# Hybrid attention and Fourier encoder on one core: sink columns a period later, another order for the first Fourier tile, POOL for one operand, another pool for one gather

## The chip, the core and the metric

The kernel runs on one core of one Trainium2 chip. The metric is the device time of one launch in microseconds, the median of three runs. Five engines work side by side, each through its own instructions in order: PE (matrix products), ACT (scalar engine), DVE (vector engine), POOL (GpSimd) and SP, which here only issues DMAs. POOL and ACT issue some DMAs too.

## What is computed

Two sequences, 2048 and 512 positions of 1024 channels, pass through two layers and a last RMSNorm.

```python
def attention_layer(x, g, w_in, w_out, sink, rel_bias):
    h = rmsnorm(x, g); z = h @ w_in            # q, k, v, gate
    # per head: softmax over |i-j| <= 128 of q.k/8 + bias[i-j], with a sink logit in the denominator
    o = banded_gqa_with_sink(q, k, v, rel_bias, sink)
    return x + (o * silu(gate)) @ w_out

def fourier_layer(x, g, w_gate, w_out):
    h = rmsnorm(x, g)
    # per group of 256 channels: real part of the 2-D DFT over (positions, channels of the group)
    f = fftn(h in 4 groups, axes=(positions, channels), norm="ortho").real
    return x + (f * silu(h @ w_gate)) @ w_out
```

## The kernel before

**Numbers in two parts.** Every float32 operand of a matmul is kept as an upper part (a cast to fp32r, made by ACT) and a lower part (the rest, a subtraction by DVE or POOL). `matmul3` (line 94 carries its matmuls) adds three products of them into one bank of PSUM. `split` makes both parts of a tile.

**Attention.** The 2560 positions are worked off in five chunks of 512; chunk 0 is the short sequence. In a chunk, eight pairs of heads follow each other. A period, `n` in `range(17)`, covers half a pair: the scores of a new half (`scores`, L451), the transposes (`transp`, L509, tile `pt`), casts (`parts`, L517 on ACT and L518 on DVE, tile `pts`) and the product with v (`av`, L535) of the half before, with projections of later pairs (`qp`, `gp`) placed in between as filler for PE. The order inside a period is written out by hand: `seq` chains the instructions of PE, ACT and DVE in the order of the program, and `after` ties others to an anchor. A scheduler decides the rest of the order at build time; at run time each engine goes through its instructions strictly in that order.

At every even period `at[n // 2 + 1].start()` takes a bias tile `b` for the next pair: SP loads its 384 middle columns from `rowd` (L426), and at once ACT copies the negated sink logits into its first and last column (L431). The next instructions of ACT are casts of `pts`. DVE reads the tile first two periods after `start`, when it adds bias and scores (`biased`, L470). `out_evac` copies the upper half of the av result with ACT (L544, tile `t`) and finishes it with DVE and POOL (L553 to L559). `extra(i)` then issues side work, among it the squares of the next chunk's rows (L161). In chunk 0 the weights come in float32 (`w32q`, `w32g`, `w32o`) and are split on ACT (L113) and POOL (L118).

**Fourier layer, first part.** The 20 tiles of 128 positions are taken in pairs of tiles. For a pair (class `Pair`), `norms` squares and scales a tile, `turn` transposes half of it (L972), `own` and `parts` make the two parts, `sums` forms the sums of a Strassen-like scheme, `z` (L94, L1022) and `z_odd_even` (L1036, L1043) multiply by the channel DFT. `gates` then forms seven products with parts of the gate weights in three PSUM accumulators W, Z and X: B11, then X with `b21`, T1, T2, B22, T3 and N4; behind each, `hooks` do steps of the next pair. The first pair (tiles 16 and 17) has no pair ahead of it, so its steps stand by themselves behind the rest of the attention phase (`tail`): `turns1` and `turns2` (both tiles transposed, tile 17 first), `turns3`, `turns4`, `z_odd_even` of tile 17, `z` of tile 16. `build` loads `w32N` and splits it into N4 and T3, both lower parts on DVE (L914).

**Fourier layer, second part.** `position` forms the DFT over positions for two mirrored residues at a time, multiplies by the gate (`s2`, L1294) and gives two row tiles `u`. `gated` loads the gate rows: by SP, or for the mirrored residue by an indirect gather that POOL issues (L1243), into a tile of the pool `x` (four buffers, `xtile`). The last residues 1, 7, 3 and 5 go through class `Outs`; while `products` of one multiplies by the output weights, its hooks `split_g`, `transform` and `turns` prepare the next. `f_sums("N4", left)` loads four weight tiles into the pool `L` (20 buffers, `left`).

Of the kernel before, what the change touches and what calls it, by code (L numbers as in the profile page):

```python
# [37 lines left out]
def f32(ap):  # L38
    return ap.bitcast(F32)
# [3 lines left out]
def encoder(  # L43
# [97 lines left out]
    def attention_phase():  # L141

        with ExitStack() as es:
# [274 lines left out]
            def attention(c, p, res, uTs):  # L418
# [5 lines left out]
                def start():  # L424
                    bt = ap.tile([P, 2, 386], F32, tag="bias", bufs=2, name=f"b{c}_{p}")
                    SP.dma_start(  # L426
                        bt[:, :, 1:385],
                        bass.AP(rowd.tensor, rowd.offset + p * 1024, [[1, P], [512, 2], [1, 384]]),
                    )

                    ends = ACT.copy(bt[:, :, 0:386:385], sk[:, 2 * p : 2 * p + 2, None].to_broadcast([P, 2, 2]))  # L431
                    if p:
                        seq(ACT, ends)
                    st["bias"] = bt
                    uT = wp.tile([P, 2, CH], F32R, align_bytes=LINE, tag="uT", bufs=8, name=f"uT{c}_{p}")
                    uTs.append((uT[:, 0], uT[:, 1]))
                    st["uT"] = uT

                def span(b):
                    gb = tok // P + b  # L440
# [123 lines left out]

                    return split

                return start, scores, biased, exps, divide, transp, parts, av, out_evac

            def out_proj(c, uTs):
                tok = CHUNKS[c][0]  # L570
# [56 lines left out]
                steps.append(lambda: evac(1))  # L627
                return steps

            Heads = namedtuple("Heads", "start scores biased exps divide transp parts av out_evac")  # L630

            def pieces(out, a, b, op):

# [133 lines left out]
            for c in range(len(CHUNKS)):  # L767

                if c > 1:
                    hs, halo = make_h(c, invb)  # L770
                for s in tail:
                    s()
                if c == 1:
                    hs, halo = make_h(c, invb)
                if c:
                    invb0 = kv_proj(c, hs, halo)
                else:
                    invb0 = kv_proj(c, hs, halo, first_norms, early)
                rowd, sk = bias
                uTs = []  # L780
                res = [{} for p in range(8)]
                at = [Heads(*attention(c, p, res[p], uTs)) for p in range(8)]
                loads, work = [], []
                for p in range(8):
                    load, steps = qg_proj(c, p, hs, res[p], invb0)
                    loads.append(load)
                    work += steps
                loads[0]()
                at[0].start()

                ahead_n = 16 if c == 0 else 12
                chain.pop(PE, None)
                for s in work[:8]:
                    s()
                loads[1]()
                for s in work[8:ahead_n]:
                    s()

                m = 15 * KD - ahead_n
                quota = [m * (i + 1) // 27 - m * i // 27 for i in range(27)] + [4, 4]  # L800
                assert sum(quota) == len(work) - ahead_n
                work = work[ahead_n:]
                op = out_proj(c, uTs)
                split = None

                def extra(i):
                    nonlocal norm_steps, invb, inv
                    if c + 1 < len(CHUNKS):
                        if i == 24:
                            norm_steps = stats(c + 1)  # L810
                        if i >= (38 if c else 24) and i % (2 if c else 4) == 0 and norm_steps:
                            inv = norm_steps.pop(0)()
                        elif i == 56:
                            invb = spread(c + 1, inv)
                    if c in EXTRA and i in EXTRA[c]:
                        EXTRA[c][i]()
                    if c == len(CHUNKS) - 1 and i in AHEAD:
                        AHEAD[i]()
                    if c == 0 and i % 8 == 3 and 1 <= i // 8 < 3:
                        load_w(0, LATE[i // 8 - 1], f"late{i // 8}", late=last_exp[0])  # L820

                fourth = bank(f"s{c}")
                zeros(fourth)
                for n in range(17):
                    new = (at[n // 2], 2 * (n % 2)) if n < 16 else None
                    old = (at[(n - 1) // 2], 2 * ((n - 1) % 2)) if n else None
                    if n % 2 == 0 and n < 14:
                        at[n // 2 + 1].start()
                    if n % 2 and n // 2 + 2 < 8:
                        loads[n // 2 + 2]()  # L830
                    chain.setdefault(PE, None)

                    if new:
                        new[0].scores(new[1], spt[:2])
                    if old:
                        for b in range(2):
                            old[0].transp(old[1] + b)
                    if new:
                        for j in range(2):
                            new[0].biased(new[1], j)  # L840
                        new[0].scores(new[1] + 1, (spt[2], spt[0] if n else fourth))
                    if n == 15:

                        for j in range(2):
                            new[0].biased(new[1] + 1, j)
                    if old:
                        for b in range(2):
                            old[0].parts(old[1] + b)
                    if new:
                        for j in range(2):  # L850
                            new[0].exps(new[1], j)
                    if split and c:
                        split()
                        split = None
                    if new:
                        if n < 15:
                            for j in range(2):
                                new[0].biased(new[1] + 1, j)
                        while late:
                            late.pop()()  # L860
                        new[0].divide(new[1], 0)
                        for j in range(2):
                            new[0].exps(new[1] + 1, j)
                        new[0].divide(new[1], 1)
                        for j in range(2):
                            new[0].divide(new[1] + 1, j)
                    for i in range(quota[2 * n] if n < 15 else 18 - n):
                        (work or op).pop(0)()
                    if split:
                        split()  # L870
                        split = None
                    if old:
                        old[0].av(old[1])
                        split = old[0].out_evac(old[1])
                    for i in range(4 * n, 4 * n + 4):
                        extra(i)
                    if n == 16:
                        split()
                    half = quota[2 * n + 1] if n < 14 else 4 if n == 14 else 2
                    for i in range(half):  # L880
                        (work or op).pop(0)()
                chain.pop(PE)
                if c == len(CHUNKS) - 1:

                    for i in range(2):
                        op[i]()
                        op[i] = lambda: None
                tail = op
            return tail

    def fourier_phase(tail):
        with ExitStack() as es:
# [18 lines left out]
            def split(t, src, lo_engine=DVE):  # L911

                ACT.copy(t[:, 0], src)
                lo_engine.tensor_tensor(t[:, 1], src, f32(t[:, 0]), ALU.subtract)  # L914
                return t[:, 0], t[:, 1]

            def split_T(src, name, flip=False):
# [205 lines left out]
            def take(w32, k, place, *names):  # L1123

                for w, half in sorted(zip(names, range(2))):
                    wg[w][k] = split(place([P, 2, 512], F32R, f"w{w}_{k}"), w32[:, half])

            def build(k):
                w32 = right([P, 2, 512], F32, f"w32N_{k}")
# [70 lines left out]
            kept = []  # L1200

            pr = pairs[0]
            turns1(pr)
            turns2(pr)
            turns3(pr)
            turns4(pr)
            more()
            more()
            pr.z_odd_even()
            for hf in range(2):  # L1210
                pr.z(hf)
            for k in range(4):
                build(k)
            for n, pr in enumerate(pairs[:-1]):
# [391 lines left out]
            for k1, k2 in ((7, 3), (3, 5), (5, None)):  # L1606
# [1 line left out]
                gl, tb = nxt["r"]  # L1608

                def split_g():  # L1610
                    nxt["s"] = [gated(name, r, xtile) for r in tiles]
                    if not ft["N4"]:

                        f_sums("N4", left)
                    nxt["p"] = [halves_of(name, *gl, hf) for hf in range(2)]

                def transform(third):
                    nxt["o"] = Outs(k1, position(name, k1, None, None, tiles, (nxt["s"], tb), nxt["p"], third))

                def turns():  # L1620
# [109 lines left out]
```

## Time and profile before

| | |
|---|---|
| median of 3 runs | 1607.7 us (1604.67 to 1608.85) |
| profiled execution | 1608.11 us, span 1606.3 us |
| PE busy | 1586.9 us (99%) |
| DVE, ACT, POOL busy | 1141.7, 880.3, 438.2 us |
| DMA | 373.90 MB, 233 GB/s mean |
| mean granted PE clock | 0.997 |

Busy time is the time in which an engine has an instruction running; ends of matmuls are modelled, so short stops of PE may not show in it. In the timelines of the profile a row gives start, duration, engine, line, operation, tiles (out<-in), shape and count, and in brackets the idle time before it with what ended it. Buffer numbers are left out of the names: `trb` is any transpose bank of the first Fourier part, `jkb` the scratch output of a square, `x` a row tile.

### The profile page before, as it was taken

The page shows a single profiled execution, that of the slowest core. Times are in us where ns is not written, and L with a number is a line of the kernel's source. Part 1 is how long each engine was busy: PE and PEld are TensorE (multiplying, and loading weights), DVE is VectorE, ACT ScalarE, POOL GpSimd, SP SyncE. Part 2 cuts the span into 40 slices and gives each one's busy share as a digit, 9 for nine tenths or more (in the row PEclk, how much of TensorE's full clock was granted, in tenths as well). Part 3 has the DMA queues.
Part 4 walks back from the last instruction along what each step waited for, and adds up shares of the span by engine and source line. Part 5 has one row for each costly group of instructions (what it writes and reads, how often), then busy time and mean ns, then how long its engine had stood idle before and what let it go on. Part 6 is the DMA issues. An engine that isn't in the chain of part 4 may idle for free.

```text
span 1606.3 us, 27426 instructions
## 1 busy us (share of the span) xinstructions
PE 1586.9 (99%) x9755; PEld 1322.6 (82%) x9755; DVE 1141.7 (71%) x2779; ACT 880.3 (55%) x2107; POOL 438.2 (27%) x605
## 2 busy tenths in 40 slices
PE   9999999999999999999999999999999999999998
PEld 7776888888898888988888888878888887888886
DVE  6787665777538776377764577668878877888696
ACT  6687634677237674257752476646655554343352
POOL 2466561421403414024222242211112121100010
PEclk9999999999999999999999999999999999999999
DMA  7577696655765576756659656656657569455952
GB/s 291 207 286 263 226 349 233 227 220 205 289 230 191 206 257 235 251 194 229 238 164 334 211 208 222 243 201 225 217 203 248 184 224 407 166 185 206 352 192 92
DMA packets 100580, 373.90 MB, mean 233 GB/s; under 512 B 12139, under 2 KB 22379, under 8 KB 83036
## 3 DMA queue, kind: packets, MB, share of 16 engines
q1 hardware_dynamic: 81708, 297.91, 52.4%
q0 software_dynamic: 16400, 70.04, 11.3%
q10 hardware_dynamic: 2336, 4.20, 0.7%
q8 instruction: 78, 1.28, 0.3%
q14 instruction: 58, 0.48, 0.1%
HBM read 280.84 MB, written 91.26 MB: 232 GB/s over the span
## 4 chain that ended last, share of the span: by engine, by line
PE 83%; DMA 7%; DVE 5%; ACT 2%; issue 1%; POOL 1%; SPq 0%; POOLq 0%; DVEq 0%; ACTq 0%
PE qp L94 13%; PE gp L94 12%; PE op L94 9%; PE spt L94 8%; PE spt L451 6%; PE av L535 6%; PE W L94 5%; PE fo L94 4%; PE vp L94 4%; PE pt L509 3%; PE Z L94 3%; PE Wo L94 2%; PE X L94 1%; PE z L94 1%; DMA b<-rowd 1%
## 5 line engine op out<-in xcount | busy, mean ns | idle before, releaser
L470 DVE CUSTOM_DVE_ANT_0 S<-spt,b 128x385 f32<-128x385 f32 (+1 forms) x315 | 154.2, 528 | 121.1 <-PE spt L451 120.8
L94 PE MATMUL qp<-h,wq 128*128 128x512 f32 x960 | 238.6, 398 | 0.0
L94 PE MATMUL gp<-h,wg 128*128 128x512 f32 x960 | 237.4, 395 | 0.0
L94 PEld LDWEIGHTS gp<-h,wg 128*128 128x128 f32 x960 | 174.9, 188 | 43.3 <-issue 9.7
L94 PEld LDWEIGHTS qp<-h,wq 128*128 128x128 f32 x960 | 175.9, 189 | 41.8 <-issue 5.5
L478 ACT ACTIVATE S<-S 128x385 f32<-128x385 f32 (+1 forms) x320 | 190.3, 606 | 18.4 <-DVE S L470 17.0
L517 ACT CAST pts<-pt 128x384 fp32r<-128x384 f32 (+1 forms) x320 | 123.8, 472 | 131.1 <-PE pt L509 130.8
L518 DVE TENSOR_TENSOR pts<-pt,pts 128x384 fp32r<-128x384 f32 (+1 forms) x320 | 147.6, 523 | 34.5 <-ACT pts L517 33.6
L94 PE MATMUL op<-wo,uT 128*128 128x512 f32 x600 | 140.4, 391 | 0.0
L94 PE MATMUL fo<-wo,tTu 128*128 128x512 f32 x576 | 139.1, 392 | 0.0
L94 PEld LDWEIGHTS op<-wo,uT 128*128 128x128 f32 x600 | 111.9, 188 | 23.9 <-issue 0.7
L451 PE MATMUL spt<-kwin,qab 64*128 64x384 f32 (+1 forms) x945 | 129.5, 356 | 0.0
L559 POOL TENSOR_TENSOR uT<-o,uT 128x256 fp32r<-128x256 f32 x75 | 55.6, 741 | 250.5 <-ACT uT L558 246.2
L94 PEld LDWEIGHTS fo<-wo,tTu 128*128 128x128 f32 x576 | 106.3, 188 | 20.3
L535 PEld LDWEIGHTS av<-pts,v 128*128 128x128 f32 x576 | 101.0, 188 | 24.0 <-ACT pts L517 3.7
L535 PE MATMUL av<-pts,v 128*128 128x512 f32 (+1 forms) x576 | 117.0, 342 | 3.3 <-ACT pts L517 2.6
L451 PEld LDWEIGHTS spt<-kwin,qab 64*128 64x128 f32 x945 | 84.2, 185 | 29.9 <-issue 21.5
L490 DVE TENSOR_SCALAR S<-S 128x384 f32<-128x384 f32 (+1 forms) x192 | 91.4, 476 | 6.4
L555 POOL TENSOR_TENSOR o<-o,s 128x256 f32<-128x256 f32 x75 | 55.3, 738 | 134.4 <-DVE o L553 134.1
L94 PE MATMUL spt<-wo,uT 128*128 128x512 f32 x360 | 86.7, 392 | 0.0
L94 PEld LDWEIGHTS spt<-wo,uT 128*128 128x128 f32 x360 | 66.5, 188 | 13.7
L509 PEld LDWEIGHTS pt<-ident,S 64*128 64x128 f32 x1792 | 68.2, 138 | 5.2 <-issue 2.3
(317 smaller groups left out, 2985.8 us busy)
## 6 DMA issues: line engine op xcount, KB each, us to landing
wo<-wsd SPq DMA_DIRECT2D x32, 1024.0 KB, 5.9
wq<-wsd SPq DMA_DIRECT2D x31, 1024.0 KB, 7.6
wg<-wsd SPq DMA_DIRECT2D x31, 1024.0 KB, 5.1
x<-x1d SPq DMA_DIRECT2D x40, 512.0 KB, 3.7
b<-b21d SPq DMA_DIRECT2D x40, 512.0 KB, 6.5
b<-rowd SPq DMA_DIRECT2D x40, 384.0 KB, 4.3
xs<-in_x_dram SPq DMA_DIRECT2D x23, 512.0 KB, 6.7
s2d<-gt POOLq DMA_DIRECT2D x40, 256.0 KB, 3.2
```

The source lines that it names most:

```text
L94: pe(PE.matmul(out, a[i], b[j], start=start and i + j == 0, stop=stop and i == 1, skip_group_check=more))
L451: pe(PE.matmul(banks[j][:, 2 + k0 * P : 2 + k1 * P], res["q"][rows, qp, b * P : (b + 1) * P], kwin[g][rows, kp, b * P + k0 * P : b * P + k ...
L470: seq(DVE, DVE.tensor_tensor_reduce(out=s[:, e0:e1], in0=ps[:, 1 + e0 : 1 + e1], in1=st["bias"][:, j, 386 - e1 : 386 - e0][:, ::-1], scale ...
L478: last_exp[0] = seq(ACT, ACT.activation(s[:, e0:e1], s[:, e0:e1], AF.Exp, bias=s[:, 386:387], scale=-1.0, accum_out=s[:, 387:388]))
L490: seq(DVE, DVE.tensor_scalar(s[:, ks], s[:, ks], den, None, ALU.mult))
L509: pe(PE.transpose(ps[h][:, kb, j, :], ss[j][rows, 1 + kb * P : 1 + (kb + 1) * P], ident[rows, rows]))
L517: seq(ACT, ACT.copy(hi, ps[:, k0:k1]))
L518: seq(DVE, DVE.tensor_tensor(lo, ps[:, k0:k1], f32(hi), ALU.subtract))
L535: pe(PE.matmul(to, v, pt, start=n == part == 0, stop=part == 1 and n in (1, len(todo) - 1), skip_group_check=n > 1,))
L555: eng.tensor_tensor(o, o, s, ALU.mult)
L559: low = eng.tensor_tensor(lo, o, f32(hi), ALU.subtract)
```

## The change

Four edits. The sink copy leaves `start` and becomes a step of its own, `sinks`, which runs in the odd period after `start`, behind `out_evac` and ahead of `extra`. The first pair of the Fourier layer transposes tile 16 and forms its `z` ahead of tile 17's steps. The lower parts of N4 are made by POOL in two pieces each. In `split_g` the second tile of residue 7 comes from the pool `L`, and `f_sums("N4", left)` moves from `split_g` to `transform`.

```diff
@@ attention
-                    ends = ACT.copy(bt[:, :, 0:386:385], sk[:, 2 * p : 2 * p + 2, None].to_broadcast([P, 2, 2]))
-                    if p:
-                        seq(ACT, ends)
...
+                def sinks():
+                    ends = ACT.copy(
+                        st["bias"][:, :, 0:386:385], sk[:, 2 * p : 2 * p + 2, None].to_broadcast([P, 2, 2])
+                    )
+                    if p:
+                        seq(ACT, ends)
@@ ahead of period 0
                 at[0].start()
+                at[0].sinks()
@@ in period n
                         split = old[0].out_evac(old[1])
+                    if n % 2 and n < 15:
+                        at[n // 2 + 1].sinks()
                     for i in range(4 * n, 4 * n + 4):
                         extra(i)
@@ split
-                lo_engine.tensor_tensor(t[:, 1], src, f32(t[:, 0]), ALU.subtract)
+                for cs in (slice(0, 256), slice(256, 512)) if lo_engine is POOL else (slice(0, 512),):
+                    lo_engine.tensor_tensor(t[:, 1, cs], src[:, cs], f32(t[:, 0, cs]), ALU.subtract)
@@ take
-                    wg[w][k] = split(place([P, 2, 512], F32R, f"w{w}_{k}"), w32[:, half])
+                    wg[w][k] = split(place([P, 2, 512], F32R, f"w{w}_{k}"), w32[:, half], POOL if w == "N4" else DVE)
@@ first pair
             pr = pairs[0]
+            for hf in range(2):
+                pr.turn(0, hf)
+            for hf in range(2):
+                pr.z(hf)
             turns1(pr)
-            turns2(pr)
+            for i in (2, 4):
+                pr.sums(i)
+            pr.parts(1)
+            pr.parts(2)
             turns3(pr)
             turns4(pr)
             more()
             more()
             pr.z_odd_even()
-            for hf in range(2):
-                pr.z(hf)
@@ split_g, transform
                 def split_g():
-                    nxt["s"] = [gated(name, r, xtile) for r in tiles]
+                    places = (xtile, xtile if ft["N4"] else left)
+                    nxt["s"] = [gated(name, r, place) for r, place in zip(tiles, places)]
+                    nxt["p"] = [halves_of(name, *gl, hf) for hf in range(2)]
+
+                def transform(third):
                     if not ft["N4"]:
                         f_sums("N4", left)
-                    nxt["p"] = [halves_of(name, *gl, hf) for hf in range(2)]
-
-                def transform(third):
```

More of the change, by code (lines that the diff above doesn't have):

```diff
@@ L565, in out_evac @@
                     return split
-                return start, scores, biased, exps, divide, transp, parts, av, out_evac
+                return start, sinks, scores, biased, exps, divide, transp, parts, av, out_evac
             def out_proj(c, uTs):
@@ L628, in out_proj @@
                 return steps
-            Heads = namedtuple("Heads", "start scores biased exps divide transp parts av out_evac")
+            Heads = namedtuple("Heads", "start sinks scores biased exps divide transp parts av out_evac")
             def pieces(out, a, b, op):
```

## The prediction

> **What bounds the kernel now.** I read the page first, then the list of waits of PE, then windows of 20 us, then the timeline where PE stops.
>
> ```profile
> span 1606.3 us, 27426 instructions
> ...
> PE 1586.9 (99%) x9755; PEld 1322.6 (82%) x9755; DVE 1141.7 (71%) x2779; ACT 880.3 (55%) x2107; POOL 438.2 (27%) x605
> ```
>
> PE is busy for 1586.9 of 1606.3 us, and the change takes no matmul away. So only time in which PE stands still, or runs at a lower clock, can be won: 19.4 us of idle time at the most, plus the clock. The waits of PE, longest first:
>
> ```profile
> PE av L535 <- ACT pts L517: 2.6, 2, 1.8
> PE z L1036 <- ACT S L913: 1.8, 1, 1.8
> PE pt L509 <- DVE o L553: 1.2, 2, 0.8
> PE tr L1337 <- DVE up L1294: 1.2, 1, 1.2
> ...
> PE av L535 <- DVE pts L518: 0.6, 2, 0.3
> ```
>
> The columns are the total in us, how often, and the longest. Three places matter: the softmax of chunk 0 (av and pt), the first tile of the Fourier layer (z), and the transposes of a late output position (tr). The windows show a second price:
>
> ```profile
> core 0: us, PE busy (x) PEld busy (x) DVE busy (x) ACT busy (x) POOL busy (x), PEclk, DMA share, GB/s
> ...
> 140.00:160.00 20.00, 17.90 (x97) 13.63 (x94) 14.59 (x50) 14.13 (x36) 14.77 (x22) 0.91 0.75 258
> ...
> 1060.00:1080.00 20.00, 18.18 (x90) 15.10 (x88) 11.67 (x19) 2.43 (x5) 3.92 (x7) 1.00 0.36 119
> 1080.00:1100.00 20.00, 19.78 (x107) 17.21 (x106) 16.25 (x29) 15.42 (x31) 1.10 (x2) 0.91 0.78 277
> ```
>
> In two windows the granted clock is 0.91 instead of 1.00, each time directly after a stop of 1.8 us. 0.09 of 20 us is 1.8 us of PE time. A stop of that length costs about twice itself.
>
> **Part 1, sink columns.** ACT fills two columns of each bias tile with a copy that waits for the bias DMA, and everything behind it on ACT waits too.
>
> ```profile
> ACT b L431 <- DMA b<-rowd: 55.6, 32, 4.5
> ```
> ```profile
> 107.84 0.36 SPq L110 DMA_DIRECT2D w32q<-in_w_in_dram  x1
> ...
> 118.65 1.05 ACT L113 CAST wq<-w32q 128x1024 fp32r<-128x1024 f32 x1 [0.79 <-DMA w32q<-in_w_in_dram]
> ...
> 123.47 0.38 SPq L426 DMA_DIRECT2D b<-rowd  x1
> 126.38 0.33 SPq L110 DMA_DIRECT2D w32q<-in_w_in_dram  x1
> ...
> 130.85 0.20 ACT L431 COPY b<-sk 128x4 f32<-128x4 f32 x1 [3.63 <-DMA b<-rowd]
> 137.88 1.04 ACT L113 CAST wq<-w32q 128x1024 fp32r<-128x1024 f32 x1
> 142.94 0.43 SPq L426 DMA_DIRECT2D b<-rowd  x1
> 144.11 2.91 PE L94 MATMUL gp<-h,wg 128*128 128x512 f32 x12
> 151.10 0.20 ACT L431 COPY b<-sk 128x4 f32<-128x4 f32 x1 [4.49 <-DMA b<-rowd]
> ...
> 153.73 0.50 PE L535 MATMUL av<-pts,v 128*128 128x512 f32 x1 [1.82 <-ACT pts L517]
> 155.55 4.49 PE L94 MATMUL qp<-h,wq 128*128 128x512 f32 x12
> ```
>
> In all but two of the 32 waits the cost is nil, because PE has projections queued meanwhile. In chunk 0 twice it is not: ACT stands 3.63 us until 130.85 and 4.49 us until 151.10, its casts of the probabilities (pts, queued right behind) come late, and PE stops. The copy moves one period later on ACT, behind the next period's evacuation of av. The slowest landing took 8.2 us (142.94 to 151.10), and between two bias issues lie 19.5 us (123.47 to 142.94), of which the copy now leaves the DMA nearly all. So the wait goes entirely. The copy itself (0.20 us) stays one instruction; the tile is first read in the period after it, so nobody new waits for it. The DMA issue stays where it was on SP.
>
> Gain: av 2.6 and 0.6, and of pt the larger stop, 0.8 (ACT's backlog from the first wait), together 4.0 us. The other pt stop comes earlier and stays. Clock: twelve qp matmuls took 4.49 us where twelve gp took 2.91, so 1.6 us more. Given back: what is late next is the cast of wq. Its load took 10.8 us once (107.84 to 118.65); issued at 126.38, it is there at 137.2 by that, and ACT, no longer held up 3.63 us, would come well before that. So ACT gains only 0.7 us on 137.88 there, while PE, without its stops of 0.8 + 0.3 + 0.8, comes 1.9 us earlier for the next av: a stop of at most 1.2 us, of which I take 1.0 (0 if the load is quicker; 1.7 if the same lateness stops PE twice more by a few tenths). **Sum 4.0 + 1.6 - 1.0 = 4.6 us**, bounds 3.5 and 6.
>
> **Part 2, first tile ahead in the Fourier layer.**
>
> ```profile
> 1075.96 1.91 PE L972 MATMUL trb<-ident,x 128*128 128x128 f32 x16
> ...
> 1076.59 0.59 ACT L995 COPY s<-trb 128x512 f32<-128x512 f32 x1 [16.72 <-PE trb L972]
> ...
> 1079.69 0.50 PE L1036 MATMUL z<-chan_sb,S 128*128 128x256 f32 x2 [1.82 <-ACT S L913]
> ...
> 1086.96 3.03 PE L94 MATMUL z<-chan_sb,tTb 128*128 128x256 f32 x24
> 1087.03 1.06 ACT L939 ACTIVATE jkb<-x 128x1024 bf16<-128x1024 f32 x1
> ...
> 1089.65 1.28 DVE L964 SCALAR_TENSOR_TENSOR x<-x,invb,g1b 128x1024 f32<-128x1024 f32 x1 [0.73 <-POOL invb L88]
> ...
> 1092.81 1.03 PE L972 MATMUL trb<-ident,x 128*128 128x128 f32 x8
> 1093.82 0.68 DVE L914 TENSOR_TENSOR wN<-w32N,wN 128x512 fp32r<-128x512 f32 x1
> ```
>
> Before, PE does 16 transposes and then waits 1.82 us, because z of tile 17 needs the chain copy, sum, cast. After (order of the built program), tile 16 is transposed first; its z needs only a cast. Counting from the first transpose: 8 transposes 0.95 us; the cast begins at 0.63 (1076.59 - 1075.96) and ends at 1.22, so PE waits 0.3 us; 24 z matmuls 2.9; 8 transposes 0.95; twelve B11 matmuls 2.75 (0.23 apart, as gp at 144.11): 7.85. Then, interleaved, six X (1.4), sixteen z of tile 17 (1.9) and twelve T1 (2.75): 13.9. T2 needs W copied out. That copy stands on ACT behind nine DVE steps of 0.6 to 0.7 us from 6.3 on (to 12.0), then a cast, the square of x1_19 (1.06) and a cast: ready at 14.9. **A new wait of 1.0 us.** Four T2 matmuls later, at 15.8, PE needs tile 19 normalised: square done at 13.8, DVE free at 15.0, POOL to 15.7, norm 1.28, so 17.0: **a new wait of about 1 us.** Before, those transposes stood at 16.85 (1092.81 - 1075.96), but after has seven more matmuls (1.6 us) done by then. So the tile wins 1.5 us net, of 1.82 plus 1.8 of clock; I take off 0.5 for z of tile 19, which waits for evacuations one place later on ACT: **1.0 us**. SP: x1_18's load is moved behind one load of w32N, 0.5 us of issue, hidden because ACT reaches its square later than before.
>
> **Part 3, POOL for the lower parts of N4.** DVE loses four instructions of 0.68 us (2.7 us); POOL gains eight.
>
> ```profile
> L559 POOL TENSOR_TENSOR uT<-o,uT 128x256 fp32r<-128x256 f32 x75 | 55.6, 741 | 250.5 <-ACT uT L558 246.2
> ```
> ```profile
> 213.25 3.10 POOL L206 TENSOR_TENSOR xk<-xk,invb 128x640 f32<-128x640 f32 x2
> 213.48 3.42 DVE L211 SCALAR_TENSOR_TENSOR h<-xk,g0s,h 128x512 fp32r<-128x512 f32 x1 [6.60 <-ACT h L210]
> ```
> ```profile
> L211 DVE SCALAR_TENSOR_TENSOR h<-xk,g0s,h x40: 737/748/4343, 6.6 to 857.1; 128x512 fp32r<-128x512 f32 x40
> ```
>
> 8 x 0.741 = 5.9 us on a POOL that is busy for 1.1 of 20 us there; N4 is the last product of the gates, so its lateness is covered. But a DVE instruction with both operands in SBUF took 3.42 us instead of the median 0.748 while two POOL instructions ran: it ended only after both. POOL's first pair starts when POOL has given the inverse norm of tile 19, just when DVE's norm wants to start: up to 2 x 0.74 = 1.5 us on the wait above. The Trainium skill (SBUF — State Buffer, "Who interferes with whom") says that a DVE instruction with two SBUF inputs and a GpSimd instruction that reads SBUF block each other wholly, whoever issues first; by this rule the part costs 0 or 1.5 us with nothing between, and the 3.42 us agree. Bounds: a gain of 1 (DVE relieved of 2.7) and a loss of 1.5 us here, 5.9 if all four pairs come first. I take 0: DVE waits for a semaphore, POOL does not, but DVE saves as much later.
>
> **Part 4, the gather.**
>
> ```profile
> 1496.95 0.61 POOL L1232 DMA_DIRECT2D tbp<-in_tabs_dram  x1
> ...
> 1514.69 1.00 POOL L1243 DMA_INDIRECT s2p<-s2d,mir  x1 [5.08 <-DMA out_dram<-x]
> ...
> 1523.39 1.22 DVE L1294 TENSOR_TENSOR up<-up,s2p 128x1024 f32<-128x1024 f32 x1 [3.10 <-DMA s2p<-s2d,mir]
> ...
> 1524.76 1.50 PE L1337 MATMUL tr<-ident,up 128*128 128x128 f32 x12 [1.21 <-DVE up L1294]
> ```
>
> The gather waited until 1514.69 for a buffer that an output store held, landed at 1523.39, and PE stopped 1.21 us. In the other pool a buffer is free, and POOL issues it right behind the table load of 1496.95, ahead of a norm's power that comes 12 us later. With the same 8.7 us it lands by 1507. The table of the next position takes a buffer later, but is read only in the next product. **1.2 us**, bounds 0.8 and 1.5.
>
> **Sum.** 4.6 + 1.0 + 0 + 1.2 = 6.8 us. The profiled execution took 1608.1 us (span 1606.3 and 1.8 around it): 1601.3. The median of the runs shown is 0.4 lower, so **1600.9 us**. What a measurement here can tell from no change is 0.3%, 4.8 us.
>
> **Rivals.**
> - The clock falls in the first tile again: its two new waits, 2 us within 3 us, resemble the stop of 1.82 that was followed by 0.91. Price 1.7: 1602.6; with POOL ahead of the norm as well (1.5), 1604.1. For it speaks that together they are as long; against, that they are two, and that the single stop of 1.21 at 1524.76 left the clock at 1.00. Chance 0.30.
> - The low clock is not the stops' doing and stays in both places: 1.6 + 1.8 back, 1604.3. Against it: the only two low windows follow the only two stops of 1.8. The Trainium skill (TensorE: Matmul & The Clock Gate, "What's actually happening") lets the clock halve after at least one idle window of about 3.4 us, and no stop here is that long; this trace disagrees. Chance 0.05.
> - The edits do half of what they say: chunk 0 loses its stops to w32q and w32o loads instead (3.5 us less): 1604.4. DMA is at 0.75 there. Chance 0.10.
> - Slower: POOL's pairs get in ahead of DVE each time. All four at 1.5 us are 5.9 us on the chain that PE follows in the first tile, which with the 3 us of new waits makes two low-clock stretches (3.4): 12.3 against the 3.6 removed, 8.7 lost, 5.8 won elsewhere, so 1610.6. It decides from a POOL share at which DVE's two-SBUF instructions of that stage mostly take over 1.4 us. POOL's casts arrive spread out, which speaks against. Chance 0.05.
>
> **Numbers.** The forecast has 0.50. Its own range is 1597.5 (part 1 with 6, drains between matmuls counted) to 1602.5. Eight in ten reach from 1596.5 to 1605.0. Faster by over 0.3%, below 1602.9: the forecast (0.50) and two thirds of the first rival, those without the POOL term (0.20), 0.70. Within 0.3%, up to 1612.5, lie the rest of it, the next two rivals and most of the slower one, 0.28; slower 0.02.
>
> **What would show it.** Right: no ACT wait for b, no av stop over 1 us in chunk 0, window 140 to 160 at clock 1.00, no tr stop at L1337's line, z of tile 16 before tile 17, POOL some 6 us busier near 1090. Wrong: a 0.91 that stays near 1080, a norm of tile 19 of 2.8 us, new av stops near 140.

## The result, and the profile after

| | before | after |
|---|---|---|
| median of 20 runs each, side by side | 1607.03 us (1603.82 to 1609.26) | 1609.29 us (1607.55 to 1612.08) |
| ratio, 95% interval | | 1.0016 (1.0009 to 1.0022) |
| profiled execution, span | 1608.11, 1606.3 us | 1608.66, 1606.9 us |

The change makes the kernel slower by about 2.3 us. The forecast was 6.8 us faster. The first lines of the page, after:

```profile
span 1606.9 us, 27447 instructions
...
PE 1588.0 (99%) x9755; PEld 1322.9 (82%) x9755; DVE 1138.7 (71%) x2775; ACT 879.1 (55%) x2107; POOL 445.9 (28%) x613
```

PE has the same 9755 matmuls and is busy 1.1 us longer. POOL has eight instructions more and 7.7 us more work, as the edit of N4 says. The waits of PE after the change (total in us, times, longest):

```profile
PE Ap L94 <- DVE gp L1270: 2.1, 2, 1.9
PE spt L94 <- ACT h L210: 1.5, 1, 1.5
PE idle L232 <- DVE idle L229: 1.2, 1, 1.2
PE trb L980 <- DVE x L972: 1.0, 1, 1.0
PE W L94 <- ACT c L1097: 1.0, 1, 1.0
PE As L94 <- ACT us L1303: 0.6, 1, 0.6
PE av L539 <- ACT pts L521: 0.5, 1, 0.5
```

All three places that the forecast wanted to clear are clear: av has 0.5 us left of 2.6, the stop of z and the stop of the transposes `tr` are gone. In their place stand gp (1.9 us in one stop, at a product where PE did not stop before), trb and W (1.0 us each, both forecast). The stop of spt lies at 6.88 us, ahead of every edit. The windows of 20 us (the same columns as in the prediction):

```profile
140.00:160.00 20.00, 18.95 (x127) 14.59 (x126) 17.22 (x64) 17.13 (x47) 16.23 (x24) 1.00 0.86 315
...
1080.00:1100.00 20.00, 17.80 (x92) 14.04 (x91) 17.77 (x28) 15.66 (x32) 7.57 (x8) 1.00 0.57 210
1500.00:1520.00 20.00, 18.09 (x85) 15.32 (x84) 11.50 (x21) 6.53 (x15) 0.57 (x2) 0.91 0.95 349
```

The clock of 0.91 has left 140 and 1080 and has come up at 1500, behind the new stop.

Where the time went is best read from how far a kernel is ahead of before's profiled execution at the same matmul (start in one trace less start in the other, both from the span's start; the places are times of before). All numbers are us, positive is ahead:

| profiled kernel | 161 | 1030 | 1062 | 1320 | 1486 | 1598 |
|---|---|---|---|---|---|---|
| after | 4.89 | 2.15 | 2.14 | 1.68 | 1.68 | -0.55 |
| sinks_only | 4.90 | 1.53 | 1.53 | 2.20 | 1.42 | 0.93 |
| sinks_before_t | 4.67 | 4.88 | 4.84 | 7.00 | 6.93 | 6.09 |
| sinks_chunk0 | 5.11 | 5.14 | 5.09 | 5.70 | 5.69 | 5.78 |
| tile_only | 1.04 | 0.89 | 0.84 | 0.85 | 0.60 | 0.45 |
| n4_only | 0.06 | -0.06 | -0.10 | -0.10 | -0.16 | -0.19 |
| gather_only | -0.54 | -1.00 | -1.00 | 0.20 | 0.17 | -0.27 |
| after_no_gather | 4.52 | 1.97 | 1.93 | 0.45 | 0.27 | 0.14 |
| sinks_t_gather_late | 4.19 | 2.81 | 2.81 | 4.93 | 4.86 | 6.30 |

After wins 4.9 us in chunk 0, loses 2.7 in many small steps through chunks 1 to 4, 0.5 in the first part of the Fourier layer (1062 to 1320), and 2.2 at the gather. The other rows are the experiments, told below.

### The profile page after: what moved, and what is told of

Its sections match the earlier page's. It is cut to its first block, busy times and chain, and to the rows that moved or that the text cites. A ratio compares the mean times of both kernels' runs of the same rounds, so it can differ in the third digit from the quotient of the medians.

```text
span 1606.9 us, 27447 instructions
## 1 busy us (share of the span) xinstructions
PE 1588.0 (99%) x9755; PEld 1322.9 (82%) x9755; DVE 1138.7 (71%) x2775; ACT 879.1 (55%) x2107; POOL 445.9 (28%) x613
## 4 chain that ended last, share of the span: by engine, by line
PE 83%; issue 5%; DVE 4%; DMA 3%; POOL 2%; ACT 2%; POOLq 0%; DVEq 0%; SPq 0%; ACTq 0%
PE gp L94 13%; PE qp L94 13%; PE op L94 9%; PE spt L94 8%; PE spt L455 6%; PE av L539 6%; PE fo L94 5%; PE W L94 4%; PE vp L94 4%; PE pt L513 3%; PE Wo L94 2%; PE Z L94 2%; DMA w32q<-in_w_in_dram 1%; PE z L94 1%; PE Zo L94 1%
```

## The experiments

### Each edit alone

Four kernels, each with one edit of the diff and the rest as before. Ratios are given against before's runs on the same chip.

> Before with the sink columns a period later and nothing else. Theory: two opposite effects. Chunk 0 gains about 5 us (the stops of PE near 140 and 153 and the half clock behind the second go), and chunks 1 to 4 give back about 2.6 us, 0.08 us for each of 32 pairs, since the first bias addition of a new pair on DVE now waits for ACT too, beside PE and the bias DMA, and frees its score bank about 0.1 us later. Net 2.4 us faster (ratio 0.9985), and the lead of PE over before falls steadily from about 5 us at 161 us to about 2.4 us at 1030 us. Rival: the loss in chunks 1 to 4 is not from the sinks; then the lead stays at 5 us and the ratio is 0.997.

> Before with the first tile of the Fourier layer ahead, lower parts of N4 still on DVE. Theory: the stop of 1.8 us and the half clock behind it go (3.5 us), but new stops at the copied W, at the transposes of tile 19 and at z take about 3 us in their place; within 1 us of before (ratio 0.9995 to 1.0005). Rival: what the changed kernel lost in this tile came from the lower parts on POOL; then this kernel alone is 1.5 to 2 us faster (0.999), with a stop at the transposes of tile 19 well under 1 us.

> Before with the lower parts of N4 on POOL in two pieces, the order of the first tile as before. Theory: nothing, within 0.5 us (ratio 0.9997 to 1.0003), POOL busy 6 us longer. Rival: a DVE instruction of this stage that reads two operands from SBUF is held while POOL works, 0.7 to 1.5 us each time; then 1 to 1.5 us slower, and a norm of over 2 us is in the trace.

> Before with the gather of residue 7 in the other pool and nothing else. Theory: the gather, issued near 1498, shares the DMA with the two loads of g for residue 7 that the next product needs; these take over 9 us instead of 7.3, PE stops about 1.9 us at the first product with gp and runs at half clock for 3.4 us behind it (1.7 us), while the stop of 1.2 us at the transposes goes: 2.4 us slower (ratio 1.0015). Rival: the late gp was only a meeting of this edit with the others' lead; then the stop at the transposes goes and nothing takes its place, 1.2 us faster (0.9993).

| kernel | median (11 runs; before 33) | ratio, 95% interval |
|---|---|---|
| before, same chip | 1607.9 | |
| sinks_only | 1605.92 | 0.9987 (0.9978 to 0.9996) |
| tile_only | 1608.88 | 1.0008 (0.9999 to 1.0017) |
| n4_only | 1608.69 | 1.0004 (0.9995 to 1.0013) |
| gather_only | 1607.71 | 0.9994 (0.9985 to 1.0003) |

Only the sinks stand clear of no change, and with 2.0 us between the medians they give less than half of the forecast's 4.6. The lead falls from 4.9 to 1.5 us in chunks 1 to 4 although nothing but the sink copy has moved there. Most of this loss belongs to the edit; 0.7 us of it is a single step near 801 us, where ACT waits 3.1 us for a load of the next chunk's rows (2.4 in before) and PE's next products come later by as much. The other three are each within their interval of nothing. For gather_only the two theories stood at 1.0015 and 0.9993; the time speaks for the second, the trace for the first: the stop at gp is there (1.69 us), the one at `tr` gone, but the clock stayed at 1.00, so the exchange cost 0.4 us between 1486 and 1598 instead of after's 2.2.

### The third wait of DVE

In the built programs the first bias addition of most pairs (`S<-spt,b` on DVE) waits for PE and the bias DMA before the change, and for PE, the DMA and ACT after it. Two kernels test whether that is the loss: one has the copy one place earlier on ACT, ahead of `t`, for which DVE waits anyway; the other keeps the old place in chunks 1 to 4. Their edits are shown against sinks_only.

```diff
# sinks_before_t
                     old[0].av(old[1])
+                    if n % 2 and n < 15:
+                        at[n // 2 + 1].sinks()
                     split = old[0].out_evac(old[1])
-                if n % 2 and n < 15:
-                    at[n // 2 + 1].sinks()
# sinks_chunk0
                 at[n // 2 + 1].start()
+                if c:
+                    at[n // 2 + 1].sinks()
...
-                if n % 2 and n < 15:
+                if n % 2 and n < 15 and c == 0:
                     at[n // 2 + 1].sinks()
```

> Before with the sink columns a period later, but one place earlier on ACT than in the changed kernel: ahead of the copy t of av, not behind it. DVE waits for t in any case, so its first bias addition of a pair needs no wait for ACT of its own. Theory: the loss in chunks 1 to 4 comes from that third wait; here the lead of 4.9 us at 161 us is still over 4.3 us at 1030 us, and the kernel is 4 to 4.5 us faster (ratio 0.9973). Rival: the loss comes from the copy's place in the odd period as such (ACT's evacuation or casts come 0.2 us later); then the lead falls here too, to about 2 us, and the ratio is 0.9987.

> Before with the sink columns a period later in chunk 0 alone, the old place in chunks 1 to 4. Both theories of the loss in chunks 1 to 4 expect the lead of 4.9 us at 161 us to stay within 0.4 us up to 1030 us and a ratio of 0.9973. If the lead falls by over 1 us all the same, the loss has nothing to do with the sinks.

Measured: sinks_before_t 1602.78 us, 0.9975 (0.9966 to 0.9984); sinks_chunk0 1603.49 us, 0.9976 (0.9966 to 0.9986); before on that chip 1607.38. Both keep their lead (4.7 to 4.9, and 5.1 to 5.1). One more kernel has the copy ahead of t, sinks_t_gather_late (below), and its lead does fall, from 4.2 to 2.8. But 1.1 of these 1.4 us are the same single step near 801 us, where ACT waits 3.4 us for that load, and it has none of the small steps, one a pair, that after, sinks_only and after_no_gather show. Between sinks_only and sinks_before_t lies one swap of two neighbours on ACT, and 1.2 thousandths of the time.

The traces show the mechanism. First before, then after, then sinks_before_t: the answers for the bias addition's line in chunks 1 to 4 (duration in ns, least, median and most), then one pair on PE and DVE.

```profile
L470 DVEq EVENT_SEMAPHORE  x31: 21/21/21, 262.2 to 1018.7; - x31
```
```profile
912.08 0.78 PE L451 MATMUL spt<-kwin,qab 64*128 64x384 f32 x6
...
912.90 0.56 DVE L470 CUSTOM_DVE_ANT_0 S<-spt,b 128x385 f32<-128x385 f32 x1 [1.99 <-PE spt L451]
...
913.30 1.01 PE L451 MATMUL spt<-kwin,qab 64*128 64x384 f32 x6
```
```profile
L474 DVEq EVENT_SEMAPHORE  x34: 21/2543/2694, 272.7 to 1016.5; - x34
```
```profile
909.33 0.78 PE L455 MATMUL spt<-kwin,qab 64*128 64x384 f32 x6
...
910.26 0.56 DVE L474 CUSTOM_DVE_ANT_0 S<-spt,b 128x385 f32<-128x385 f32 x1 [2.10 <-PE spt L455]
...
910.54 1.12 PE L455 MATMUL spt<-kwin,qab 64*128 64x384 f32 x6
```
```profile
L474 DVEq EVENT_SEMAPHORE  x30: 21/21/21, 288.2 to 1013.9; - x30
```
```profile
907.23 0.78 PE L455 MATMUL spt<-kwin,qab 64*128 64x384 f32 x6
...
908.05 0.56 DVE L474 CUSTOM_DVE_ANT_0 S<-spt,b 128x385 f32<-128x385 f32 x1 [1.99 <-PE spt L455]
...
908.45 1.01 PE L455 MATMUL spt<-kwin,qab 64*128 64x384 f32 x6
```

Some waits of the addition are served by EVENT_SEMAPHORE instructions (they do nothing but wait) of DVE's queue ahead of it. Before, these had nothing left to wait for (21 ns). After, they sit for a median of 2543 ns: the really long wait, the one for the scores, is served there now. The traces' semaphore records name the score matmul as what ended 28 of the 34; in before and in sinks_before_t they name it for none. In the pair shown the addition then starts 0.93 us after the first score matmul (910.26 less 909.33) instead of 0.82 (912.90 less 912.08). The scores' bank comes free 0.11 us later, and the next six score matmuls take 1.12 us instead of 1.01. Seven pairs in each of four chunks make 28, and 28 additions of after start later by 0.09 to 0.11 us: 2.7 / 28 is 0.10 us a pair, in sinks_only, without the single step, 2.7 / 28 too. So it is not a late copy that costs, but the extra wait. The Trainium skill (Perfetto Trace Analysis, "Identifying Dependency Chains") says that instructions that wait on several engines may have EventSemaphore instructions put in front of them; the rows agree, and 0.09 to 0.11 us is what it costs here.

### The gather

after_no_gather is the changed kernel with `split_g` and `transform` as before. sinks_t_gather_late is sinks_before_t with the gather in the pool `L`, as changed, but released late: ACT writes one column of its tile (the gather overwrites it) behind the last cast of gp. Its edit is shown against the changed kernel.

```diff
# sinks_t_gather_late
-                    nxt["s"] = [gated(name, r, place) for r, place in zip(tiles, places)]
+                    nxt["s"] = [gated(name, tiles[0], xtile)]
                     nxt["p"] = [halves_of(name, *gl, hf) for hf in range(2)]
...
+                    nxt["s"].append(gated(name, tiles[1], left, f32(nxt["p"][1][1][:, 0, 0:1])))
# gated(name, r, place, late=None)
                 s2 = place([P, D], F32, f"s2{name}_{r[0]}")
+                if late is not None:
+                    ACT.copy(s2[:, 0:1], late)
```

> As the run with the sinks ahead of t, and with the gather of residue 7 in the other pool but released late: ACT writes one column of its tile behind the last cast of gp, and the gather waits for that, so it is issued near 1511 us instead of 1497. Theory (the early gather takes DMA time from the loads of g): these land within 7.5 us again, no stop over 0.4 us at the product with gp, the gather lands near 1520, no stop over 0.4 us at the transposes; 1.2 us faster than the run with the sinks ahead of t (ratio 0.9966). Rival (the order of the casts on ACT and DVE, not the landing, makes gp late): the stop of 1.7 to 1.9 us at gp stays, and the ratio is 0.998.

> The changed kernel with the gather as before. Theory: the stop at gp (1.9 us, with 1.7 us of half clock where it falls) goes, the stop of 1.2 to 1.4 us at the transposes comes back: 0.5 to 2.4 us faster than the changed kernel, so level with before or 1 us faster (ratio 0.9993 to 1.0012, and above the run with the sinks alone, 0.9987, by what the first tile and POOL cost). Rival: the gather's part is nothing; ratio 1.0016 as the changed kernel.

Measured: sinks_t_gather_late 1601.77 us (7 runs), 0.9967 (0.9956 to 0.9979), the lowest median of all and clearly ahead of before, though its interval overlaps that of sinks_before_t; after_no_gather 1607.41 us, 1.0002 (0.9993 to 1.0011), so without the gather's edit the change is neither faster nor slower. The timeline of after at the stop:

```profile
1496.19 1.28 POOL L1256 DMA_INDIRECT s2p<-s2d,mir  x1 [0.30 <-issue]
...
1498.37 1.14 SPq L1604 DMA_DIRECT2D go<-god  x2
...
1507.58 0.62 ACT L1269 CAST gp<-go 128x512 fp32r<-128x512 f32 x1 [6.05 <-DMA go<-god]
...
1511.99 1.89 DVE L1270 TENSOR_TENSOR gp<-go,gp 128x512 fp32r<-128x512 f32 x3
...
1512.72 0.71 PE L94 MATMUL Ap<-gp,tbp 128*128 128x260 f32 x2 [1.91 <-DVE gp L1270]
...
1514.52 3.73 PE L94 MATMUL Wo<-fT,S 128*128 128x512 f32 x12
```

The gather leaves 2.2 us ahead of the two loads of g. Their row in the list of DMAs of that stage (issues, KB each, median us to landing), for before, after, gather_only and sinks_t_gather_late:

```profile
go<-god SPq DMA_DIRECT2D x2, 512.0 KB, 7.3
```
```profile
go<-god SPq DMA_DIRECT2D x2, 512.0 KB, 9.4
```
```profile
go<-god SPq DMA_DIRECT2D x2, 512.0 KB, 9.2
```
```profile
go<-god SPq DMA_DIRECT2D x2, 512.0 KB, 7.4
```

With the early gather they land after 9.2 and 9.4 us. In the profiles without it the time varies, 7.3 in before, 7.5 in after_no_gather and 8.1 in sinks_before_t, which has a stop of 0.5 us at gp; so the early gather costs the loads 1.1 to 2.1 us. Issued behind them, at 1506.01 in its trace (near 1511 was expected), the gather leaves them alone (7.4), the stop at gp is gone, and the stop at `tr` is gone too. So the landing, not the order of casts, made gp late. The DMAs had next to nothing to spare there even in before, with its share of 0.96:

```profile
1500.00:1520.00 20.00, 20.00 (x100) 16.99 (x100) 15.14 (x28) 7.56 (x17) 2.15 (x3) 1.00 0.96 351
```

## Why the prediction was wrong

**Part 1.** In chunk 0 it was right against before's profile: forecast 4.6, measured 4.9. The 1.6 us of clock in it were partly luck: of the four profiles with the old chunk 0, tile_only has the stops and no low clock behind them, and is 1.0 us ahead of before at 161. No stop of av over 0.54 us is left, the clock there is 1.00, and the cast of wq now waits for its DMA, as said:

```profile
137.46 1.05 ACT L113 CAST wq<-w32q 128x1024 fp32r<-128x1024 f32 x1 [2.31 <-DMA w32q<-in_w_in_dram]
```
```profile
140.94 1.79 PE L539 MATMUL av<-pts,v 128*128 128x512 f32 x6 [0.54 <-ACT pts L521]
```

ACT's wait for b did not go entirely: five of the 32 waits are left, 7.4 us, one in each chunk, where the first pair's copy still stands right behind its load.

The step that failed is "the tile is first read in the period after it, so nobody new waits for it". The copy is done in time, but one reader gets a wait more, once a pair; its price was left out, 2.7 us.

**Part 2.** The new stops came nearly as worked out: 1.01 us for W (forecast 1.0), 1.05 for tile 19 (about 1).

```profile
1089.07 1.20 PE L94 MATMUL W<-wT,S 128*128 128x512 f32 x4 [1.01 <-ACT c L1097]
...
1091.31 1.10 PE L980 MATMUL trb<-ident,x 128*128 128x128 f32 x8 [1.05 <-DVE x L972]
```

Two other terms failed. The first is the 1.8 us of clock, counted as always there. Of the seven profiled executions that have the old order, all have the stop of 1.82 us at z, but only two (before, sinks_chunk0) a low clock behind it. The other five, with the old order too, are 1.5 us further ahead of before at 1100 than at 1062. The new order gives 0.9 by then (tile_only) or 0.5 (after). So against an ordinary execution it loses 0.6 to 1.0 us up to there.

The second term is the 0.5 us taken off for what comes behind. Between 1100 and 1140 the lead falls by 1.5 us in tile_only and in after, in several stops of 0.2 to 0.6 us at W and z. Of the old order's five, two lose nothing there (sinks_before_t, sinks_t_gather_late). Three lose 1.0 to 1.8, with a stop of 1.0 to 1.2 us at W instead of 0.2: in sinks_only and gather_only ACT had waited 1.14 and 0.85 us for the load of a row tile, in n4_only POOL's pieces had held DVE up (part 3). So the edit trades a stop of 1.8 us for several that sum to as much or more. A loss of about 1 us is likely, but tile_only's interval does not settle it.

**Part 3.** Taken as 0; after is 0.4 us behind tile_only at 1100, inside the bounds given. The norm of tile 19 and the next subtraction, after, and in tile_only, where DVE has the lower parts of N4:

```profile
1089.44 2.40 POOL L922 TENSOR_TENSOR wN<-w32N,wN 128x256 fp32r<-128x256 f32 x2
1089.49 1.76 DVE L972 SCALAR_TENSOR_TENSOR x<-x,invb,g1b 128x1024 f32<-128x1024 f32 x1 [0.74 <-POOL invb L88]
1091.18 1.22 DVE L922 TENSOR_TENSOR wT<-w32N,wT 128x512 fp32r<-128x512 f32 x1
```
```profile
1090.79 1.28 DVE L964 SCALAR_TENSOR_TENSOR x<-x,invb,g1b 128x1024 f32<-128x1024 f32 x1 [0.73 <-POOL invb L88]
...
1092.59 0.68 DVE L914 TENSOR_TENSOR wT<-w32N,wT 128x512 fp32r<-128x512 f32 x1
```

POOL's pair did start at that moment, but held the norm up by 0.48 us, not 1.5, and the subtraction by 0.54. It did not get in as a pair: POOL's first piece took 0.74 us and the second 1.70, until 1091.84, while the norm ended at 1091.25 and the subtraction only at 1092.40. So the two engines took turns, and "nothing between" 0 and 1.5 us did not come out.

That this was nothing on the whole, because "DVE saves as much later", is not shown. In n4_only's trace a norm (1.75 us) and three subtractions (1.16 to 1.23) are held up in the same way, and between 1100 and 1120 it loses 1.8 us of lead; sinks_before_t, level with it until that norm, loses nothing there. This is one execution, and n4_only's interval allows no loss as well as one of 2 us. The slower rival, which needed over 1.4 us each time, did not come.

**Part 4.** The gather did land near 1506 and the stop of 1.21 us went. What failed is that only POOL's queue and the buffers were followed, not the transfers that SP issues right behind it: the loads of g, for which the next product waits. Forecast +1.2, measured -2.2.

**The sum.** 4.9 - 2.7 - 0.5 - 2.2 is -0.5; the spans differ by 0.6. The medians differ by 2.3. Part of the other 1.7 us lies in the profiled executions. Before's had two low clocks ahead of the kernel's end: its mean granted clock is 0.9968 in the trace, and before's 62 runs beside the experiments average 0.9977 and 0.9982 on their two chips. The difference, times 1606 us, is 1.4 to 2.2 us. After's profile has 0.9973 and its 20 runs average 0.9977, which is 0.6 us. So the low clocks of the two profiled executions can be 0.8 to 1.6 us of the 1.7; the rest stays open.

**The rivals.** The kernel is slower by 0.16%, within the 0.3% that was called no change; that outcome had 0.28, and 0.02 stood for a loss of over 0.3%. That the edits do half of what they say was given for another reason (DMA loads in chunk 0), and chunk 0 kept its gain. The first rival, the low clock back in the first tile, did not happen in after's profile but did in after_no_gather's, with the same instructions in that tile; the price there was 1.0 us (its lead falls by 1.48 us from 1062 to 1320, after's by 0.46), not 1.7. The second, that the low clock is not the stops' doing, fell: see the last section.

## What to carry to other kernels

When a producer moves to a later place, look at the wait list of each reader, not only at when the data is there: put ahead of something that the reader waits for anyway, the copy cost nothing here. Where the DMAs are nearly always busy (0.95 here), an earlier transfer takes its time from those beside it, so name the load that the next product needs before issuing anything ahead of it. A stop seen with a low clock behind it in one profile is worth at most its own length, and the clock only as often as it falls; other executions of the same instructions tell how often.

## What the runs showed of the hardware

The low clock comes, but for the kernel's last microseconds, in pieces of 3.41 us (3413 ns in the traces' clock records) at exactly 0.50, on a fixed grid: the two of before start at 155.78 and 1080.79, and 925.01 us is 271.0 times 3.413. Windows laid on that grid in three kernels, each pair the window with the stop and the one behind it (us and length, PE, PEld, DVE, ACT, POOL busy, PEclk, DMA share, GB/s), first before, then gather_only, then after_no_gather:

```profile
1077.38:1080.79 3.41, 1.37 (x10) 0.92 (x9) 3.05 (x5) 2.43 (x6) 0.30 (x1) 1.00 0.95 253
1080.79:1084.20 3.41, 3.41 (x15) 3.02 (x14) 2.66 (x5) 1.90 (x6) 0.00 (x0) 0.50 0.95 381
```
```profile
152.19:155.60 3.41, 1.24 (x4) 0.67 (x4) 2.28 (x7) 3.02 (x10) 2.74 (x4) 1.00 0.91 381
155.60:159.01 3.41, 3.41 (x10) 2.75 (x9) 3.07 (x14) 3.40 (x8) 1.39 (x4) 0.50 0.61 169
1077.19:1080.60 3.41, 1.68 (x16) 1.44 (x14) 2.52 (x4) 2.15 (x4) 1.22 (x3) 1.00 0.83 269
1080.60:1084.01 3.41, 3.10 (x18) 2.68 (x19) 3.40 (x7) 2.84 (x8) 0.00 (x0) 1.00 0.96 342
1510.68:1514.09 3.41, 1.72 (x11) 1.31 (x9) 2.66 (x5) 1.42 (x3) 0.56 (x1) 1.00 0.63 259
1514.09:1517.50 3.41, 3.41 (x19) 3.00 (x20) 2.99 (x7) 0.93 (x3) 0.00 (x0) 1.00 1.03 311
```
```profile
1088.49:1091.90 3.41, 1.57 (x7) 1.05 (x8) 2.68 (x5) 2.80 (x6) 2.77 (x3) 1.00 0.90 307
1091.90:1095.31 3.41, 3.41 (x13) 2.93 (x12) 2.65 (x4) 2.10 (x4) 1.62 (x4) 0.50 1.03 413
```

Windows in which PE is busy for 1.24, 1.37 and 1.57 of 3.41 us are followed by half clock; those with 1.68 and 1.72 are not. The border lies near half of the window (before's first low clock, behind a window with 1.77 us busy by modelled ends, is the one case on the wrong side; in n4_only 1.62 us busy were followed by half clock too). So a stop of 1.8 us halves the clock when it falls into one window and not when a border cuts it: the stop at z did the first in before and sinks_chunk0; in sinks_only, n4_only, sinks_before_t and sinks_t_gather_late a border cut it, and in gather_only a border cut off its last 0.09 us, which was enough. And two stops of 1 us in one window do it too (after_no_gather), while in after the border fell between them. The Trainium skill (TensorE: Matmul & The Clock Gate, "What's actually happening") gives the window as 3413 ns and free-running; the traces agree. It asks for an idle window before the clock halves; here windows in which PE stood idle for 1.8 to 2.2 of the 3.41 us were enough.
